# Three held chunks of the expert table turned by VectorE instead of TensorE

## The chip, the cores and the metric

The kernel runs on one core of a Trainium2 chip. The core has five engines, each with its own instruction queue worked strictly in order: TensorE (PE in the profile; its weight loads are PEld), VectorE (DVE), ScalarE (ACT), GpSimd (POOL) and SyncE (SP, which here only issues transfers). Transfers (DMAs) run beside them on 16 DMA engines; those that SP and ACT issue use hardware queues (q1 and q10), those of POOL a software queue (q0). The metric is the device time of one execution in microseconds, compared by medians of several executions on one chip.

## The reference

One decoder layer on 256 tokens of width 1024. The part before the experts (norm, one wide projection, retention, block attention, gates, output projection) is only touched by this change at its end. What matters is the expert step (PEER):

```python
def peer(h, w_q, sub_keys, u_tab, v_tab):
    q = (ht @ w_q).reshape(T, PEER_HEADS, 2, half)
    s = jnp.einsum('thcd,hcnd->thcn', q, sub_keys)
    s1, i1 = lax.top_k(s[:, :, 0], PEER_TOPK)
    s2, i2 = lax.top_k(s[:, :, 1], PEER_TOPK)
    ...                                   # 256 sums per token and head, top 16 of them
    gates = jax.nn.softmax(top_s, axis=-1)
    u = u_tab[ec]                         # 16384 experts, rows of 1024 numbers
    a = jax.nn.gelu(jnp.einsum('td,thkd->thk', hc, u), approximate=False)
    return jnp.einsum('thk,thkd->td', gc * a, v_tab[ec])
```

Each token needs 8 heads x 16 experts out of 16384. Everything is float32.

## The kernel before, in words

The program is written out in the order in which each engine is to work; nothing is reordered later. It has four stages.

**Mixer (to about 245 us).** The dense part of the layer, as a list of weight pieces of 512 KB. For piece i, SP loads it into a ring of six buffers (`raw_ring`), ACT and DVE cut it into a high and a low part (`cut`, L151 and L152), and PE multiplies (`products`). During this stage 28 of the 128 chunks of the expert table u (128 experts each, 512 KB) are already prepared: POOL loads a chunk as four quarters of its columns (`load_quarters`, L738, four DMAs of 128 KB each), DVE turns it with two block transposes (`turn`, L742), and ACT's queue stores it turned to memory (`turned`). These are the chunks in `EARLY`.

**Queries (about 245 to 300 us).** 16 more pieces, of `peer_w_q`, go through the same ring, cut three pieces ahead of their products. After every fourth piece the epilogue `queries(q)` runs: ACT copies the result (L612), PE multiplies it with the sub-keys (L625), ACT copies the scores (L629), and a top-k job for each half of the tokens is put on a list (`chain`), whose steps DVE works off in small portions between the cuts: `MAX8`, `FIND_INDEX8`, `MATCH_REPLACE8` (L905 to L914) and then the choice of the best 16 sums (L939 to L993). SP loads in this stage also the 14 chunks of `HELD` (`hold`, L1160) into the part of the large tile `W` that is still free, one for each piece, and the last three after the loop. In the epilogue of the fourth query block, between ACT's copies and the sub-key products, the program turns chunks 0 and 1 by `transpose_u` (`TAHEAD` = 2).

**Stage U (about 300 to 633 us).** For each chunk c of 128 experts, PE multiplies the turned chunk with the hidden states of 128 tokens (L1321, 16 matmul records a chunk) into `acc`. A chunk that is not in `EARLY` is first turned by PE (`transpose_u`, L728: eight 128x128 transposes into PSUM, copied out by ACT, L729), two chunks ahead. Because a block transpose by VectorE leaves the columns in another order, there are two copies of the hidden states: `hTf` for chunks that PE turns, `hTd` for those that VectorE turned; `early_chunk(c)` chooses. The other tokens are served in another way: POOL gathers single rows of u by index (L1050) and DVE multiplies them out (L1061). All the top-k steps that are left run on DVE in this stage too, between those products. When the second half of the tokens is done, ACT takes exponentials of their gates (L1007), DVE normalises them (L1012 to L1014), and PE turns the indices and gates (L1210), from where on DVE builds one-hot matrices for PE (L1188, L1191, L1246, L1247).

**Stage V (633 us to the end).** The weighted sum over the table v, chunk by chunk.

At the border between mixer and queries POOL issues, in this order: the result of the mixer to memory (L571), 64 rows of the normed states to `h2x` (L599), a shift of rows inside `h2` (L600), and four DMAs that spread `h2x` into `h2y` (L604), which ACT's queue loads at the begin of stage U (L1303).

Of the kernel before, what the change touches and what calls it, by code (L numbers as in the profile page):

```python
# [25 lines left out]
D = 1024  # L26
# [23 lines left out]
TOPK = 16  # L50
HELD = [0, 1, 2, 8, 14, 21] + list(range(26, 62, 6)) + [61, 66]
HELD0 = 2
FOLD = 104
TURNED = list(range(8, 36, 2)) + [37, 40, 42, 45, 47, 50, 52, 55, 57, 60, 62, 65, 67, 70]
NPRE = len(TURNED)
# [24 lines left out]
def layer_kernel(ctx, tc, x, mix_norm_g, w_in, ret_w_branch, moba_q_gain, moba_k_gain, moba_w_branch,  # L80
# [48 lines left out]
    def add(gen, front=False):  # L129
        tasks.insert(0, gen) if front else tasks.append(gen)  # L130
# [9 lines left out]
    def pump(n=3):  # L140
        for g in list(tasks)[:n]:
            if g in tasks:
                advance(g)
# [65 lines left out]
    def cut(i, engine=V):  # L209
        if i < len(pieces):  # L210
            hi, lo = hi_tile(), lo_tile()
            split_to(hi, lo, raws.pop(i), engine)
            splits[i] = (hi, lo)
# [333 lines left out]
    def residual(j):  # L547
        def epi(o):
# [50 lines left out]
            nc.gpsimd.dma_start(h2x, h2[P - NX:])  # L599
            nc.gpsimd.dma_start(h2[NG:], h2[:NG])  # L600
            yield
            for n in range(NXG):
                src = h2x[NXP * ((n - NXV) % NXG):][:NXP]
                nc.gpsimd.dma_start(h2y[n].rearrange("h i d -> i h d"), src[:, None, :].to_broadcast([NXP, H, D]))  # L604
                yield
        return epi

    def queries(q):
        def epi(o):
# [119 lines left out]
                A.activation(u_T[c][:, 512 * q:512 * (q + 1)], p, AF.Copy)  # L729

    def early_chunk(c):
        return c in EARLY

    def load_quarters(queue, dst, c, quarters=range(4)):

        src = peer_u[0, c * P:(c + 1) * P, :].rearrange("(b a) (g d) -> g a b d", a=32, g=4)
        for g in quarters:
            queue.dma_start(dst[32 * g:32 * g + 32].rearrange("a (b d) -> a b d", b=4), src[g])  # L738

    def turn(dst, src, k):  # L740

        V.transpose(dst.rearrange("p (k b a) -> p b k a", k=KC, b=4)[:, :, k],  # L742
                    src.rearrange("p (b k i) -> p b k i", b=4, k=KC)[:, :, k])
# [410 lines left out]
    V.tensor_copy(iota4, iota[:, :, None].to_broadcast([P, NK, 4]))  # L1154
    held = list(HELD)

    def hold():
        n0, c = 1024 * (len(HELD) - len(held)), held.pop(0)
        u_raw[c] = W[:, HELD0:SCRATCH, :].rearrange("p c t -> p (c t)")[:, n0:n0 + D]
        nc.sync.dma_start(u_raw[c], peer_u[0, c * P:(c + 1) * P, :])  # L1160

    for i in range(n_mixer + 3, len(pieces)):
        load_to(i + 1)
        if held and i > n_mixer + 4:
            hold()
        products(i)
        cut(i + 3)
        pump()
        chain_step(BUDGET_Q)

# [312 lines left out]
```

## Time and profile before

| | us |
|---|---|
| median of 3 runs | 932.54 (932.08 to 933.26) |
| time of the profiled execution | 930.49 |
| its span | 928.7 |
| PE busy | 919.9 (99%) |
| DVE busy | 801.3 (86%) |
| ACT busy | 510.5 (55%) |
| POOL busy | 450.3 (48%) |
| DMA | 333.03 MB, mean 359 GB/s |

The span runs from the first to the last instruction; the time of the same execution is 1.8 us longer. In rows of the profile an operation stands as `out<-in`, with buffer numbers where a row is of one buffer alone; idle time of an engine before an instruction stands in brackets with what ended it.

### The profile page before, as it was taken

The numbers are of one execution on the slowest core, as the hardware profiler recorded it, in microseconds if no ns is written. First come the engines' busy times: TensorE is split into PE (matmuls) and PEld (weight loads), VectorE is DVE, ScalarE is ACT, GpSimd is POOL, SyncE is SP. The second block draws the span as 40 slices with busy tenths as digits, with TensorE's granted clock in tenths as the row PEclk, the third lists the DMA queues.
The fourth block names the chain that finished last, engine by engine and source line by source line (L and its number), as shares of the span: only waits on it lengthen the run. The fifth ranks groups of instructions, "written<-read, shape, count | busy, mean of one in ns | idle before, by whom it ended". The sixth has DMA issues, their size and how long they took to land.

```text
span 928.7 us, 18726 instructions
## 1 busy us (share of the span) xinstructions
PE 919.9 (99%) x6952; PEld 873.5 (94%) x6952; DVE 801.3 (86%) x1539; ACT 510.5 (55%) x938; POOL 450.3 (48%) x420
## 2 busy tenths in 40 slices
PE   9999999999999999999999999999999999999998
PEld 6877888888999999999999999999999999999997
DVE  6578766888779999999999999975998989898896
ACT  5455654544654445344677777775454545454543
POOL 3627332321202447435576787873656554455540
PEclk9999999999999999999999999999999999999999
DMA  9999989999799999999999999999999999999991
GB/s 313 214 339 337 354 282 276 345 341 325 245 381 398 404 381 352 379 379 351 405 406 405 404 383 407 395 389 348 380 405 408 409 393 410 378 409 379 386 392 56
DMA packets 108265, 333.03 MB, mean 359 GB/s; under 512 B 12460, under 2 KB 16469, under 8 KB 108046
## 3 DMA queue, kind: packets, MB, share of 16 engines
q1 hardware_dynamic: 65532, 185.17, 54.6%
q0 software_dynamic: 37824, 129.57, 38.1%
q10 hardware_dynamic: 4818, 17.09, 4.8%
q8 instruction: 55, 0.90, 0.4%
q14 instruction: 36, 0.29, 0.1%
HBM read 313.88 MB, written 19.43 MB: 359 GB/s over the span
## 4 chain that ended last, share of the span: by engine, by line
PE 93%; DMA 5%; DVE 0%; issue 0%; ACT 0%; POOL 0%; SPq 0%; DVEq 0%; ACTq 0%
PE acc L1321 24%; PE side L728 10%; PE acc L1353 10%; PE side L1353 9%; PE acc L234 6%; PE acc L235 6%; PE acc L236 6%; PE acc L1354 4%; PE side L1354 4%; DMA raw_ring<-in_w_in_dram 3%; PE acc L244 2%; PE acc L243 2%; PE acc L245 2%; PE side L1351 2%; PE acc L1351 2%; PE acc L1246 1%
## 5 line engine op out<-in xcount | busy, mean ns | idle before, releaser
L1050 POOL DMA_INDIRECT rows<-in_peer_u_dram,eg x86 | 107.9, 1255 | 72.3 <-DVE rows L1061 26.4
L1050 POOL DMA_INDIRECT rows<-in_peer_v_dram,eg x54 | 97.8, 1812 | 77.2 <-DVE vacc L1149 58.8
L728 PE MATMUL side<-ident,raw_ring 128*128 128x128 f32 x688 | 92.3, 277 | 1.1 <-DMA raw_ring<-in_peer_u_dram 1.1
L728 PEld LDWEIGHTS side<-ident,raw_ring 128*128 128x128 f32 x688 | 83.3, 192 | 1.3 <-issue 1.3
L1293 ACT ACTIVATE cw<-W 128x352 fp32r<-128x352 f32 x58 | 28.9, 498 | 74.7 <-PE acc L1354 69.2
L1195 ACT ACTIVATE oh_buf<-oh_more,tS 128x128 bf16<-128x128 f16 x176 | 58.5, 417 | 0.0
L1061 DVE SCALAR_TENSOR_TENSOR rows<-rows,h 128x1024 f32<-128x1024 f32 x44 | 55.8, 1277 | 2.6 <-DMA rows<-in_peer_u_dram,eg 1.5
L1321 PE MATMUL acc<-hTd,raw_ring 128*128 128x128 f32 x448 | 54.6, 275 | 0.0
L1149 DVE SCALAR_TENSOR_TENSOR vacc<-rows,av,vacc 128x1024 f32<-128x1024 f32 x42 | 53.7, 1278 | 0.1
L1321 PEld LDWEIGHTS acc<-hTd,raw_ring 128*128 128x128 f32 x448 | 52.3, 192 | 0.0
L1294 DVE TENSOR_TENSOR cw<-W,cw 128x352 fp32r<-128x352 f32 x58 | 30.2, 521 | 21.3 <-ACT cw L1293 20.7
L1279 POOL TENSOR_TENSOR W<-W,gl 128x256 f32<-128x256 f32 (+21 forms) x32 | 28.1, 880 | 30.7 <-ACT gl L1278 26.7
L738 POOL DMA_DIRECT2D eraw<-in_peer_u_dram x40 | 21.9, 554 | 37.7 <-DVE eT L742 37.7
L738 POOL DMA_DIRECT2D h<-in_peer_u_dram x40 | 21.8, 552 | 37.7 <-DVE hTf L742 29.6
L1191 DVE TENSOR_TENSOR oh_buf<-oh_more,tM 128x1024 f16<-128x1024 f16 x44 | 33.2, 754 | 0.0
L1188 DVE TENSOR_TENSOR oh_more<-iota,tI 128x1024 f16<-128x1024 f16 x44 | 32.8, 746 | 0.0
L1262 ACT ACTIVATE W<-acc 128x512 f32<-128x512 f32 (+22 forms) x44 | 17.4, 394 | 13.6 <-PE acc L1247 9.6
L1246 PE MATMUL acc<-oh_buf 128*128 128x128 bf16 x176 | 24.4, 219 | 0.0
L1247 PE MATMUL acc<-oh_buf 128*128 128x128 bf16 x176 | 24.4, 219 | 0.0
L1281 ACT ACTIVATE W<-acc 128x256 f32<-128x256 f32 (+21 forms) x53 | 18.4, 348 | 5.5 <-issue 3.3
L1264 DVE TENSOR_TENSOR W<-acc,W 128x256 f32<-128x256 f32 (+21 forms) x32 | 16.1, 502 | 4.6 <-ACT W L1262 4.2
L1246 PEld LDWEIGHTS <-oh_buf 128*128 128x128 f16 x176 | 19.8, 114 | 0.0
(2599 smaller groups left out, 3391.9 us busy)
## 6 DMA issues: line engine op xcount, KB each, us to landing
raw_ring<-in_peer_v_dram SPq DMA_DIRECT2D x100, 512.0 KB
raw_ring<-in_peer_u_dram SPq DMA_DIRECT2D x86, 512.0 KB
raw_ring<-in_w_in_dram SPq DMA_DIRECT2D x52, 512.0 KB
raw_ring<-turned SPq DMA_DIRECT2D x28, 512.0 KB
W<-in_peer_v_dram SPq DMA_DIRECT2D x28, 512.0 KB
raw_ring<-in_peer_w_q_dram SPq DMA_DIRECT2D x16, 512.0 KB
W<-in_peer_u_dram SPq DMA_DIRECT2D x14, 512.0 KB
eraw<-in_peer_u_dram POOLq DMA_DIRECT2D x40, 128.0 KB
```

What stands on the lines that cost most here:

```text
L234: T.matmul(o[t], xh[:, s], wh, start=(k == 0), stop=False)
L235: T.matmul(o[t], xh[:, s], wl, start=False, stop=False)
L236: T.matmul(o[t], xl[:, s], wh, start=False, stop=(k == kc - 1))
L728: T.transpose(p[:, k * P:(k + 1) * P], r.rearrange("p (i k) -> p k i", k=KC)[:, 4 * q + k], ident)
L1050: G.indirect_dma_start(out=r, out_offset=None, in_=tab, in_offset=bass.IndirectOffsetOnAxis(ap=eg[:, j:j + 1], axis=0))
L1061: V.scalar_tensor_tensor(r, r, 1.0, h, op0=OP.mult, op1=OP.mult, accum_out=av[:, j:j + 1])
L1149: V.scalar_tensor_tensor(a, r, av[:, j:j + 1], a, op0=OP.mult, op1=OP.add)
L1195: A.activation(o1[:, j], hot[:, 0, :, j], AF.Copy, scale=tS[:, t, k + j:k + j + 1])
L1246: T.matmul(p[:, j * P:(j + 1) * P], hi, o1, start=True, stop=False)
L1321: T.matmul(pa[:, n:n + NA], uT[:, k * P:(k + 1) * P], hT[:, k], start=(c % 2 == 0 and k == 0), stop=(k == KC - 1), skip_group_check=True)
L1353: T.matmul(o[b][:, :2 * ND], vh[:, n], w, start=(c == 0), stop=False, skip_group_check=True)
L1354: T.matmul(o[b][:, :ND], vl[:, n], w[:, :ND], start=False, stop=(c == NK - 1), skip_group_check=True)
```

## The change

The first three chunks of `HELD` (0, 1 and 2) become `HTURN`. They are no longer loaded whole by SP and turned by PE. POOL loads each as four quarters of columns into a scratch region of `W` (two such regions, used in turn), DVE turns it with two block transposes into the place in `W` where the held chunk stood before, and PE uses it there with `hTd`. Quarters of chunks 0 and 1 are issued before the loop over the query pieces; those of chunk 2 inside the loop, after chunk 0 has been turned out of the region. The turns stand in the loop's first three steps, right behind the cut. The four DMAs into `h2y` move from the end of the mixer to the loop's tasks, and so behind the twelve quarters on POOL's queue. `hold` runs on SP for the other eleven chunks, from the same step of the loop on, and nothing of it is left after the loop.

```diff
--- before.py
+++ after.py
@@ -50,6 +50,7 @@
 TOPK = 16
 HELD = [0, 1, 2, 8, 14, 21] + list(range(26, 62, 6)) + [61, 66]
 HELD0 = 2
+HTURN = HELD[:3]
 FOLD = 104
 TURNED = list(range(8, 36, 2)) + [37, 40, 42, 45, 47, 50, 52, 55, 57, 60, 62, 65, 67, 70]
 NPRE = len(TURNED)
@@ -599,11 +600,13 @@
             nc.gpsimd.dma_start(h2x, h2[P - NX:])
             nc.gpsimd.dma_start(h2[NG:], h2[:NG])
             yield
-            for n in range(NXG):
-                src = h2x[NXP * ((n - NXV) % NXG):][:NXP]
-                nc.gpsimd.dma_start(h2y[n].rearrange("h i d -> i h d"), src[:, None, :].to_broadcast([NXP, H, D]))
-                yield
         return epi
+
+    def spread_rows():
+        for n in range(NXG):
+            src = h2x[NXP * ((n - NXV) % NXG):][:NXP]
+            nc.gpsimd.dma_start(h2y[n].rearrange("h i d -> i h d"), src[:, None, :].to_broadcast([NXP, H, D]))
+            yield
 
     def queries(q):
         def epi(o):
@@ -729,7 +732,7 @@
                 A.activation(u_T[c][:, 512 * q:512 * (q + 1)], p, AF.Copy)
 
     def early_chunk(c):
-        return c in EARLY
+        return c in EARLY or c in HTURN
 
     def load_quarters(queue, dst, c, quarters=range(4)):
 
@@ -1154,10 +1157,29 @@
     V.tensor_copy(iota4, iota[:, :, None].to_broadcast([P, NK, 4]))
     held = list(HELD)
 
-    def hold():
+    def held_tile():
         n0, c = 1024 * (len(HELD) - len(held)), held.pop(0)
         u_raw[c] = W[:, HELD0:SCRATCH, :].rearrange("p c t -> p (c t)")[:, n0:n0 + D]
+        return c
+
+    def hold():
+        c = held_tile()
         nc.sync.dma_start(u_raw[c], peer_u[0, c * P:(c + 1) * P, :])
+
+    def held_raw(j):
+        n0 = 2048 + 1024 * (j % 2)
+        return scratch[:, n0:n0 + D]
+
+    def hold_quarters(j):
+        load_quarters(nc.gpsimd, held_raw(j), held_tile())
+
+    def hold_turn(j):
+        for k in range(0, KC, 4):
+            turn(u_raw[HTURN[j]], held_raw(j), slice(k, k + 4))
+
+    for j in range(2):
+        hold_quarters(j)
+    add(spread_rows())
 
     for i in range(n_mixer + 3, len(pieces)):
         load_to(i + 1)
@@ -1165,6 +1187,11 @@
             hold()
         products(i)
         cut(i + 3)
+        j = i - n_mixer - 3
+        if j < len(HTURN):
+            hold_turn(j)
+            if j + 2 < len(HTURN):
+                hold_quarters(j + 2)
         pump()
         chain_step(BUDGET_Q)
 
```

POOL at the border between mixer and queries, before (`h` is the tile h2, `eg<-ei` the first list of experts for the gathers; in brackets what the instruction waits for, DMASW being POOL's own transfers):

```order
L600 DMA h_75<-h_75 64x1024 [waits DMASW3_49,DMASW7_49,DMASW2_49,DMASW0_49]
L604 DMA h2y<-h2x 16x8x1024 [waits DMASW1_49]
L604 DMA h2y<-h2x 16x8x1024 x3
L983 DMA eg<-ei 64x16 [waits DMAHW1_49,DVE_49,DMAHW3_49,PE_49,DMAHW6_49,Activation_49,Pool_49]
```

The same place after the change:

```order
L601 DMA h_75<-h_75 64x1024 [waits DMASW3_49,DMASW7_49,DMASW2_49,DMASW0_49]
L741 DMA W<-in_peer_u_dram 32x4x256 [waits DMAHW2_49,DMAHW3_49,DMAHW1_49,DMAHW4_49,DMAHW0_49,DMAHW5_49,DMASW1_49,DMAHW6_49,PE_49,DMAHW7_49,Activation_49,Pool_49]
L741 DMA W<-in_peer_u_dram 32x4x256 x4
L741 DMA W<-in_peer_u_dram 32x4x256 [waits DMASW6_49]
L741 DMA W<-in_peer_u_dram 32x4x256
L741 DMA W<-in_peer_u_dram 32x4x256 [waits DMASW0_49]
L741 DMA W<-in_peer_u_dram 32x4x256 [waits DMASW1_49,DVE_49]
L741 DMA W<-in_peer_u_dram 32x4x256 [waits DMASW2_49]
L741 DMA W<-in_peer_u_dram 32x4x256 [waits DMASW3_49]
L741 DMA W<-in_peer_u_dram 32x4x256 [waits DMASW4_49]
L608 DMA h2y<-h2x 16x8x1024 [waits DMASW5_49]
L986 DMA eg<-ei 64x16 [waits DMASW1_49,DVE_49]
```

Twelve DMAs now stand between the shift of rows and the spreading into `h2y`; the ninth, the first quarter of chunk 2, waits for DVE, that is for the turn of chunk 0.

DVE at the begin of the queries, before (the cuts of three query pieces, then the first top-k step):

```order
L1154 CAST iota_2373<-iota 128x512
L152 TENSOR_TENSOR rlo__2413<-raw_ring,rhi__2412 128x1024
L152 TENSOR_TENSOR rlo__2456<-raw_ring,rhi__2455 128x1024
L152 TENSOR_TENSOR rlo__2498<-raw_ring,rhi__2497 128x1024
L905 MAX W<-W 128x8 x2
L907 MAX_INDEX W<-W 128x8 x2
```

After the change:

```order
L1157 CAST iota_2369<-iota 128x512
L153 TENSOR_TENSOR rlo__2417<-raw_ring,rhi__2416 128x1024
L745 STREAM_TRANSPOSE W<-W 128x4x4x32 x2
L153 TENSOR_TENSOR rlo__2467<-raw_ring,rhi__2466 128x1024
L745 STREAM_TRANSPOSE W<-W 128x4x4x32 x2
L153 TENSOR_TENSOR rlo__2512<-raw_ring,rhi__2511 128x1024
L745 STREAM_TRANSPOSE W<-W 128x4x4x32 x2
L908 MAX W<-W 128x8 x2
L910 MAX_INDEX W<-W 128x8 x2
```

Six transposes are put between the three cuts and the first top-k step; each pair waits for the four quarters of its chunk.

PE at the end of the queries and the begin of stage U, before:

```order
L245 MATMUL acc<-hh,rlo__2809 128x256
L728 MATMUL side<-ident,W 128x128 x16
L625 MATMUL side<-skT,W 128x128 x8
L728 MATMUL side<-ident,W 128x128 x8
L1321 MATMUL acc<-hTf,rhi__2917 128x128 x8
```

After the change:

```order
L246 MATMUL acc<-hh,rlo__2827 128x256
L628 MATMUL side<-skT,W 128x128 x8
L1348 MATMUL acc<-hTd,W 128x128 x16
L731 MATMUL side<-ident,raw_ring 128x128 x8
```

The 24 transposes of chunks 0, 1 and 2 are gone, 16 of them from between the last query product and the sub-key products.

## The prediction

> **What bounds the kernel now.** I read the page first, its busy line and the shares of its chain of waits:
>
> ```profile
> PE 919.9 (99%) x6952; PEld 873.5 (94%) x6952; DVE 801.3 (86%) x1539; ACT 510.5 (55%) x938; POOL 450.3 (48%) x420
> PE 93%; DMA 5%; DVE 0%; issue 0%; ACT 0%; POOL 0%; SPq 0%; DVEq 0%; ACTq 0%
> ```
>
> TensorE sets the end, so 24 transposes less should show in full. An average can hide a second engine that is just as late in one stage. So I read busy times by stretch next (columns: length, then busy us and instructions of PE, PEld, DVE, ACT, POOL, then granted clock, DMA share, GB/s), and the waits of PE from 245 to 640 us and of VectorE from 262 to 449:
>
> ```profile
> 251.00:262.40 11.40, 11.40 (x100) 11.40 (x100) 3.92 (x5) 7.36 (x12) 2.65 (x5) 1.00 0.74 242
> 262.40:287.40 25.00, 24.93 (x204) 24.14 (x203) 21.86 (x81) 12.58 (x16) 0.55 (x1) 1.00 1.03 404
> 287.40:357.40 70.00, 70.00 (x625) 70.00 (x624) 67.85 (x292) 30.03 (x59) 33.03 (x33) 1.00 1.00 387
> 357.40:449.00 91.60, 91.60 (x824) 91.60 (x824) 90.74 (x333) 41.76 (x83) 44.08 (x42) 1.00 0.98 370
> 449.00:633.00 184.00, 182.88 (x1794) 182.71 (x1793) 164.18 (x280) 134.40 (x378) 132.55 (x110) 1.00 1.02 396
> ...
> PE side L728 <- DMA raw_ring<-in_peer_u_dram: 1.1, 1, 1.1
> ...
> DVE sm L1012 <- ACT gates L1007: 1.8, 1, 1.8
> DVE W L905 <- ACT W L629: 1.6, 1, 1.6
> DVE rlo__2592 L152 <- ACT rhi__2591 L151: 1.3, 1, 1.3
> DVE rlo__2758 L152 <- ACT rhi__2757 L151: 1.1, 1, 1.1
> DVE rlo__2809 L152 <- ACT rhi__2808 L151: 0.2, 1, 0.2
> DVE rlo__2550 L152 <- ACT rhi__2549 L151: 0.2, 1, 0.2
> ```
>
> In the two middle rows PE is busy 70.00 of 70.00 and 91.60 of 91.60 us, but VectorE too: 67.85 and 90.74. Between the end of the queries and 449 us it has one wait worth the name, 1.8 us. Where does PE next need VectorE? At the turn of the second half's gates:
>
> ```profile
> 357.50 0.29 DVE L1012 TENSOR_REDUCE sm<-gates 128x8 f32<-128x128 f32 x1 [1.76 <-ACT gates L1007]
> ...
> 448.50 0.29 DVE L1014 TENSOR_TENSOR gates<-gates,sm 128x128 f32<-128x128 f32 x1
> 449.23 0.14 PEld L1210 LDWEIGHTS side<-ident,gates 128*128 128x128 f32 x1
> ```
>
> VectorE ends the gates at 448.50 + 0.29 = 448.79 and PE loads them at 449.23: 0.44 us of slack after 200 us of work. So there are two chains to 449 us, PE's and VectorE's, equally long within half a microsecond. The change shortens the first and lengthens the second.
>
> **What PE saves.** Its transposes and the sub-key products around them, from the chain of waits:
>
> ```profile
> 282.17 0.71 PE side L625 x4
> 282.89 1.60 PE side L625 x12
> ...
> 296.00 1.81 PE side L728 x16
> 297.81 1.79 PE side L625 x16
> 299.59 0.88 PE side L728 x8
> ```
>
> Gone are 1.81 + 0.88 = 2.69 us. The 16 transposes also covered ACT's copy of the last query block: without them the 16 products should go as in the third block, 0.71 + 1.60 = 2.31 us instead of 1.79, which gives 0.52 back. PE's gain is 2.69 − 0.52 = 2.17 us, and 2.69 if nothing is given back. ACT's six copies behind those transposes go too, on an engine 55% busy: counted as nothing.
>
> **What VectorE gets.** The block transpose costs 0.70 us, and its pairs come where these rows stand:
>
> ```profile
> 70.14 0.70 DVE L742 STREAM_TRANSPOSE hTf<-h 128x512 f32<-128x512 f32 x1
> ...
> 259.54 1.23 DVE L152 TENSOR_TENSOR rlo__2498<-raw_ring,rhi__2497 128x1024 fp32r<-128x1024 f32 x1 [1.52 <-ACT rhi__2497 L151]
> 262.40 0.49 DVE L905 MAX8 W<-W 128x8 f32<-128x128 f32 x2 [1.63 <-ACT W L629]
> 265.06 1.23 DVE L152 TENSOR_TENSOR rlo__2550<-raw_ring,rhi__2549 128x1024 fp32r<-128x1024 f32 x1 [0.22 <-ACT rhi__2549 L151]
> 269.96 1.23 DVE L152 TENSOR_TENSOR rlo__2592<-raw_ring,rhi__2591 128x1024 fp32r<-128x1024 f32 x1 [1.33 <-ACT rhi__2591 L151]
> ```
>
> Six of them are 6 x 0.70 = 4.2 us, but before 262.40 VectorE is busy only 3.92 of 11.40 us, so the work itself would fit. The price is the wait: each pair stands until its chunk has landed, and everything behind it on this engine stands too: two cuts, the first top-k step at 262.40, and so the whole row up to 449 us.
>
> Call X the time at which the third pair ends. The top-k step starts at X instead of 262.40. Of that lateness VectorE's waits in the queries can absorb 0.22 + 1.33 + 1.12 + 0.23 = 2.90 us. The 1.76 at 357.50 is absorbed as well, since ACT's exponentials there follow PE's work. And 0.44 is slack at the gates. PE is therefore later at 449 us by X − 262.40 − 2.90 − 1.76 − 0.44 = X − 267.50, but never earlier than by 2.17. Behind 449 us PE is busy 182.88 of 184.00: a shift there reaches the end.
>
> **When the third pair ends.** POOL's queue, where the quarters go, with what follows a load of the same kind in the mixer:
>
> ```profile
> 249.18 0.61 POOL L599 DMA_DIRECT2D h2x<-h  x1 [2.81 <-DVE h L578]
> 252.68 0.52 POOL L600 DMA_DIRECT2D h<-h  x1 [2.88 <-DMA h2x<-h]
> 253.19 2.13 POOL L604 DMA_DIRECT2D h2y<-h2x  x4
> ...
> 28.57 2.26 POOL L738 DMA_DIRECT2D eraw<-in_peer_u_dram  x4
> ...
> 39.02 0.71 DVE L742 STREAM_TRANSPOSE eT<-eraw 128x512 f32<-128x512 f32 x1 [1.20 <-DMA eraw<-in_peer_u_dram]
> ...
> 73.31 2.19 POOL L738 DMA_DIRECT2D eraw<-in_peer_u_dram  x4
> ...
> 83.18 0.71 DVE L742 STREAM_TRANSPOSE eT<-eraw 128x512 f32<-128x512 f32 x1 [2.64 <-DMA eraw<-in_peer_u_dram]
> ```
>
> The first quarter takes the place of the first spreading DMA, 253.2. Let g be the time from a chunk's first quarter to its last one landed. Chunk 0 is turned g1 + 1.4 us later; only then is the scratch region free and the first quarter of chunk 2 issued (the ninth quarter waits for VectorE), and chunk 2 is turned g2 + 1.4 us after that. Chunk 1, issued beside chunk 0, ends between the two. X = 253.2 + g1 + 1.4 + g2 + 1.4 = 256.0 + g1 + g2: two loads in a row, the second one behind a turn.
>
> Bounds of g, with the page's row of GB/s in 40 slices of 23.2 us:
>
> ```profile
> GB/s 313 214 339 337 354 282 276 345 341 325 245 381 398 404 381 352 379 379 351 405 406 405 404 383 407 395 389 348 380 405 408 409 393 410 378 409 379 386 392 56
> ```
>
> From below: the transfer to h2x (256 KB) held POOL from 249.18 to 252.68, 3.5 us, with little beside it; if the fourth quarter, three issues of 0.55 later, needs as much, g = 1.65 + 3.5 = 5.15. From above: the two groups of the mixer for which VectorE stood waiting took 39.02 − 28.57 = 10.45 and 83.18 − 73.31 = 9.87. Chunk 0 is loaded while transfers run at 242 GB/s (share 0.74): I take a quarter of the way from 5.15 to 9.87, 6.3. Chunk 2 is loaded at 404 GB/s (share 1.03), more than any of the first ten slices of the span, which are the mixer, so it is nearer the upper rows: three quarters of the way, 8.7. X = 256.0 + 15.0 = 271.0, and the shift at the end is 271.0 − 267.5 = **+3.5 us**. Both at the lower bound give 266.3 − 267.5 = −1.2, both at 10.45 give 276.9 − 267.5 = +9.4.
>
> [...]
>
> PE also waits inside the queries, since the later cuts come late:
>
> ```profile
> 273.58 0.28 PE L245 MATMUL acc<-hh,rlo__2550 128*128 128x256 f32 x1
> 276.46 0.28 PE L245 MATMUL acc<-hh,rlo__2592 128*128 128x256 f32 x1
> ```
>
> The cut `rlo__2550` ended at 266.29, 3.67 us behind 262.40 once its 0.22 of waiting is gone: now at 271.0 + 3.67 = 274.7, 1.1 us after PE's 273.58. `rlo__2592` comes at X + 7.24 = 278.2, 0.7 later still. That is 1.8 us lost against 2.17 gained. It doesn't add to the 3.5: PE only arrives less early at the gates, where VectorE is last anyway.
>
> **What moves at no cost.** POOL issues 12 quarters, 12 x 0.55 = 6.6 us, and stands at the ninth for chunk 0's turn to about 260.9. Behind it are four quarters and the four spreading DMAs, issued by about 265. The latter are read by ACT's queue:
>
> ```profile
> 285.99 0.55 POOL L983 DMA_DIRECT2D eg<-ei  x1 [30.67 <-ACT W L629]
> 299.69 0.33 ACTq L1303 DMA_DIRECT2D rlo__2977<-h2y  x1
> ...
> 278.45 4.22 SPq L1160 DMA_DIRECT2D W<-in_peer_u_dram  x4
> ```
>
> POOL's next own work is at 285.99 and the read at 299.69, over 30 us after the issue. Were that cover gone, every microsecond would be one of ACT's. SP drops three loads, some 1.3 us apart in its last row, so the ring's first loads of u go out some 3.8 us earlier. PE's only wait for them is the 1.1 us, which may shrink or stay. The bytes are the same.
>
> **The sum.** −2.17 on PE, overtaken by VectorE's lateness: +3.5 at the end. The profiled execution takes 930.49 us (span 928.7), which becomes 934.0. It lies 2.05 below the median of the runs, 932.54, and I carry the difference: **936.0 us**.
>
> **Rivals.** A measurement of this kernel can tell about 0.2% from no change, 1.9 us.
>
> 1. *The quarters land like lone transfers and VectorE isn't late.* For the full gain X must stay under 265.3, g1 + g2 under 9.3, 4.7 each: a little under the lower bound of 5.15. For it: the light stretch at 242 GB/s. Against it: both measured groups. Time 932.54 − 2.17 = 930.4, faster; 0.16.
> 2. *Late, but just about evened out.* g1 + g2 between 9.6 and 13.4 puts the shift between −1.9 and +1.9. The lower bounds lie here (931.3). For it speaks that nothing but POOL's loads and SP's queue competes once the spreading has moved back; against it that the second load stands in a full stretch. Time about 932.5; 0.25.
> 3. *Both loads are as slow as in the mixer.* At 10.45 each X is 276.9; `rlo__2550` then comes at 280.6, PE loses 7.7 us in the queries, and VectorE is 9.4 late at the gates: 941.9; 0.12. For it: the rows of 10.45 and 9.87; against: the first load meets few others.
>
> **Chances.** The forecast, late by 1.9 to 7 us, has 0.47; its own range is 934.4 to 939.5. With rival 3 that is 0.59 for slower by more than 0.2%; rival 2 is 0.25 for within 0.2%, rival 1 is 0.16 for faster. The range that holds 8 in 10 reaches from 930.6, nearly the full gain, to 940.5, part of the way to rival 3.
>
> **What would show it.** VectorE standing before the second transpose of a later pair, ended by the quarters of `in_peer_u_dram`, and the first top-k `MAX8` near 271 instead of 262.4. PE waiting about 1 us for `rlo` near 274. VectorE's wait at the first `L1012` (357.50) gone. PE waiting for VectorE at the second half's gates by some 4 us (VectorE 3.9 later than before, PE 0.4 earlier, 0.44 of slack). 24 fewer records of the transposes. Wrong would be: `MAX8` before 266, with PE not waiting at the gates (then rival 1), or VectorE late and the gates on time, which would mean that its work up to 449 us isn't one unbroken row as I read it.

## The result

The change makes the kernel slower: 944.10 us median (941.81 to 945.08) against 932.31 for the kernel before on the same chip, a ratio of 1.0128 with a 95% interval of 1.0115 to 1.0141. That is +11.8 us, where +3.5 was forecast and 940.5 was the upper end of the range. The profiled execution took 943.64, its span is 941.9. Of all executions on record one was in the slow state (1113.73 us at a mean granted clock of 0.753, in the run `early_whole` below), and the ratios leave it out.

The busy line and the shares of the chain of waits of the changed kernel (line numbers are up to 27 higher than before):

```profile
PE 923.2 (98%) x6928; PEld 874.5 (93%) x6928; DVE 805.4 (86%) x1545; ACT 507.4 (54%) x932; POOL 452.8 (48%) x432
PE 71%; DVE 17%; DMA 9%; issue 1%; POOL 1%; ACT 1%; SPq 0%; DVEq 0%; ACTq 0%; POOLq 0%
```

There are 24 records less on PE and 6 more on DVE, as written. But PE's busy time has risen by 3.3 us, and of the chain that ended last 17% is now DVE and 9% DMA. The three turns and the first top-k step, in DVE's timeline, and the loads they wait for in POOL's:

```profile
255.67 1.23 DVE L153 TENSOR_TENSOR rlo__2417<-raw_ring,rhi__2416 128x1024 fp32r<-128x1024 f32 x1 [3.64 <-ACT rhi__2416 L152]
264.91 1.31 DVE L745 STREAM_TRANSPOSE W<-W 128x512 f32<-128x512 f32 x2 [8.01 <-DMA W<-in_peer_u_dram]
268.55 1.30 DVE L745 STREAM_TRANSPOSE W<-W 128x512 f32<-128x512 f32 x2 [1.23 <-DMA W<-in_peer_u_dram]
275.94 1.30 DVE L745 STREAM_TRANSPOSE W<-W 128x512 f32<-128x512 f32 x2 [4.99 <-DMA W<-in_peer_u_dram]
277.17 0.45 DVE L908 MAX8 W<-W 128x8 f32<-128x128 f32 x2
```

```profile
254.45 4.38 POOL L741 DMA_DIRECT2D W<-in_peer_u_dram  x8 [0.46 <-PE acc L246]
266.51 2.18 POOL L741 DMA_DIRECT2D W<-in_peer_u_dram  x4 [7.67 <-DVE W L745]
```

The first cut here stood at 254.88 in the profile of before:

```profile
254.88 1.23 DVE L152 TENSOR_TENSOR rlo__2413<-raw_ring,rhi__2412 128x1024 fp32r<-128x1024 f32 x1 [3.63 <-ACT rhi__2412 L151]
```

So 0.8 us of the 13.2 by which the two spans differ were there before the change could delay anything: POOL's transfer to `h2x`, ahead of the first quarter, is as late (249.97 against 249.18). VectorE stands for loads for 8.01 + 1.23 + 4.99 = 14.2 us, and the top-k step comes at 277.17 instead of 262.40. Then PE's waits from 245 to 640 us, and VectorE's from 262 to 465:

```profile
PE acc L246 <- DVE rlo__2567 L153: 5.0, 1, 5.0
PE side L731 <- ACT rhi__4678 L732: 3.3, 1, 3.3
PE acc L246 <- DVE rlo__2467 L153: 0.9, 1, 0.9
```

```profile
DVE W L745 <- DMA W<-in_peer_u_dram: 14.2, 3, 8.0
DVE rows L1064 <- DMA rows<-in_peer_u_dram,eg: 3.8, 2, 2.0
```

And where the lateness reaches PE for good, the gates of the second half. In this list `DVE gates L978` is a step of the choice of the best sums, and `L1015` and `L1017` are the steps that stood at `L1012` and `L1014` before:

```profile
367.12 0.28 DVE L1015 TENSOR_REDUCE sm<-gates 128x8 f32<-128x128 f32 x1
386.82 1.23 DVE L1064 SCALAR_TENSOR_TENSOR rows<-rows,h 128x1024 f32<-128x1024 f32 x1 [1.96 <-DMA rows<-in_peer_u_dram,eg]
455.52 0.31 ACT L1010 ACTIVATE gates<-gates 128x128 f32<-128x128 f32 x1 [7.26 <-DVE gates L978]
460.21 0.29 DVE L1017 TENSOR_TENSOR gates<-gates,sm 128x128 f32<-128x128 f32 x1
460.65 0.23 PEld L1237 LDWEIGHTS side<-ident,gates 128*128 128x128 f32 x1
```

PE loads the gates at 460.65 instead of 449.23, 11.4 us later; 10.6 without the mixer's 0.8. VectorE ends them 0.15 us before that. The wait of 3.3 us that PE shows is a little earlier: ACT stood 7.26 us for VectorE before its exponentials, and its copies of turned chunks stood behind them. Behind the gates another 1.8 us are added (span 941.9 − 460.65 = 481.2 against 928.7 − 449.23 = 479.5). So the lateness takes the way that was forecast. What has to be explained is its size.

### The profile page after: what moved, and what is told of

It is laid out like the page before. It is cut to its first block, busy times and chain, and to the rows that moved or that the text cites. A ratio compares the mean times of both kernels' runs of the same rounds, so it can differ in the third digit from the quotient of the medians.

```text
span 941.9 us, 18692 instructions
## 1 busy us (share of the span) xinstructions
PE 923.2 (98%) x6928; PEld 874.5 (93%) x6928; DVE 805.4 (86%) x1545; ACT 507.4 (54%) x932; POOL 452.8 (48%) x432
## 2 busy tenths in 40 slices
DMA packets 108409, 333.03 MB, mean 354 GB/s; under 512 B 12604, under 2 KB 16613, under 8 KB 108190
## 4 chain that ended last, share of the span: by engine, by line
PE 71%; DVE 17%; DMA 9%; issue 1%; POOL 1%; ACT 1%; SPq 0%; DVEq 0%; ACTq 0%; POOLq 0%
PE acc L1348 13%; PE side L1380 9%; PE acc L1380 9%; PE acc L235 6%; PE acc L236 6%; PE acc L237 6%; PE side L731 5%; PE acc L1381 4%; PE side L1381 4%; DVE rows L1064 4%; DMA rows<-in_peer_u_dram,eg 2%; DMA raw_ring<-in_w_in_dram 2%; DMA W<-in_peer_u_dram 2%; PE side L1378 2%; PE acc L1378 2%; DVE W L966 1%
## 5 line engine op out<-in xcount | busy, mean ns | idle before, releaser
L1053 POOL DMA_INDIRECT rows<-in_peer_u_dram,eg x86 | 105.7, 1229 | 74.3 <-DVE rows L1064 29.9
L1306 POOL TENSOR_TENSOR W<-W,gl 128x256 f32<-128x256 f32 (+21 forms) x32 | 25.5, 797 | 26.7 <-ACT gl L1305 24.6
L1215 DVE TENSOR_TENSOR oh_more<-iota,tI 128x1024 f16<-128x1024 f16 x44 | 36.0, 818 | 0.0
## 6 DMA issues: line engine op xcount, KB each, us to landing
W<-in_peer_v_dram SPq DMA_DIRECT2D x28, 512.0 KB, 10.6
```

The costliest lines, as they stand in the source:

```text
L1053: G.indirect_dma_start(out=r, out_offset=None, in_=tab, in_offset=bass.IndirectOffsetOnAxis(ap=eg[:, j:j + 1], axis=0))
```

## The experiments

Each time is a median. Each ratio is against the kernel before on the same chip; intervals are 95%. The kernel before was timed anew with each group of runs: 931.51 beside `turns_no_loads`, `row_groups`, `third_region` and `late`; 932.44 beside `early_whole`, `quarters_pe`, `late_fixed` and `late_holds`; 932.11 beside `rows32`, `cols128`, `two` and `before_again`; 932.47 beside the two with another order. Code cuts below are shortened; `...` or a text in angle brackets stands for what is left out.

| run | chunks come as | turned by | time | ratio |
|---|---|---|---|---|
| the kernel before | whole | PE | 932.31 | |
| `before_again` | whole | PE | 932.05 | 0.9997 (0.9982 to 1.0011) |
| `early_whole` | whole, ahead | PE | 932.78 | 0.9997 (0.9982 to 1.0012) |
| `cols128` | quarters of columns, 128 partitions | PE | 932.56 | 1.0005 (0.9996 to 1.0015) |
| `rows32` | quarters of rows, 32 partitions | PE | 936.18 | 1.0055 (1.0038 to 1.0071) |
| `quarters_pe` | the change's quarters | PE | 938.56 | 1.0062 (1.0040 to 1.0084) |
| `turns_no_loads` | not loaded | DVE | 931.64 | 0.9998 (0.9989 to 1.0008) |
| `two` | the change's quarters, two chunks | DVE | 935.42 | 1.0036 (1.0022 to 1.0050) |
| `late` | the change's quarters | DVE, later | 937.81 | 1.0069 (1.0053 to 1.0084) |
| `late_fixed` | the change's quarters | DVE, later | 940.39 | 1.0082 (1.0061 to 1.0103) |
| `late_holds` | the change's quarters | DVE, later | 939.00 | 1.0071 (1.0046 to 1.0096) |
| `late_0213` | quarters in another order | DVE, later | 938.63 | 1.0074 (1.0058 to 1.0091) |
| `third_region` | the change's quarters, all before any turn | DVE | 940.18 | 1.0081 (1.0065 to 1.0097) |
| the change | quarters of columns, 32 partitions | DVE | 944.10 | 1.0128 (1.0115 to 1.0141) |
| `order_0213` | quarters in another order | DVE | 944.71 | 1.0129 (1.0104 to 1.0154) |
| `row_groups` | groups of rows over 128 partitions | DVE | 955.01 | 1.0252 (1.0237 to 1.0267) |

### Are the transposes the cost, or the waiting?

```diff
 def hold_quarters(j):
-    load_quarters(nc.gpsimd, held_raw(j), held_tile())
+    held_tile()
+    if j < 2:
+        G.memset(held_raw(j), 0.0)
```

> The changed kernel without the twelve quarter loads: zeros are put into the two scratch regions, and the six transposes on VectorE stay where they are, with nothing to wait for (the three chunks are left out of the result). If the lateness is VectorE standing for the loads, the transposes fall into its idle time before the first top-k step: that step starts near 263, PE keeps its 2.2 us, the time is about 930 us (2 under the kernel before, 14 under the changed one). If the transposes themselves, or their place in VectorE's row, are the cost, the first top-k step starts some 4 us later than before, 267, and the time is about 932 to 934. If the order or the new copy of the hidden states costs something of its own, it stays near 944.

Measured: 931.64 us, no difference to the kernel before, and 12.5 us under the change. VectorE's timeline:

```profile
257.19 1.22 DVE L153 TENSOR_TENSOR rlo__2411<-raw_ring,rhi__2410 128x1024 fp32r<-128x1024 f32 x1 [3.63 <-ACT rhi__2410 L152]
258.33 1.30 DVE L745 STREAM_TRANSPOSE W<-W 128x512 f32<-128x512 f32 x2
260.66 1.29 DVE L745 STREAM_TRANSPOSE W<-W 128x512 f32<-128x512 f32 x2
263.00 1.30 DVE L745 STREAM_TRANSPOSE W<-W 128x512 f32<-128x512 f32 x2
264.71 0.49 DVE L908 MAX8 W<-W 128x8 f32<-128x128 f32 x2 [0.41 <-ACT W L632]
```

The top-k step comes 264.71 − 257.19 = 7.52 us after the first cut, as before (262.40 − 254.88 = 7.52), and it still waits 0.41 for ACT. The six transposes fit into idle time and cost nothing; the whole loss hangs on the loads. In this profile PE's gain is there, and of the size that was forecast. PE loads the gates at 449.41:

```profile
449.41 0.14 PEld L1239 LDWEIGHTS side<-ident,gates 128*128 128x128 f32 x1
```

That is 449.41 − 257.19 = 192.22 us behind the first cut, against 449.23 − 254.88 = 194.35 before: 2.13 us saved, where 2.17 were forecast. But at the end of the program 1.3 us are lost again: from SP's first output transfer to the last instruction it takes 7.7 us (922.06 to 929.8), before 6.5 (922.23 to 928.7). Over the whole program, counted from the first cut, 1.2 us are saved. The timed runs, with an interval of −1.0 to +0.7 us, can't tell that from nothing. Even with loads for nothing the change as it is written would have brought hardly more than 1 us.

### Is it the second load behind the first turn?

Chunk 2 gets a raw region of its own, the place of the last held chunk:

```diff
-for j in range(2):
+for j in range(3):
     hold_quarters(j)
 def held_raw(j):
+    if j == 2:
+        return <the place of the last held chunk>
...
-    if j + 2 < len(HTURN):
-        hold_quarters(j + 2)
```

> As the changed kernel, but chunk 2 has a raw region of its own (the place of the last held chunk, which is loaded later) and its four quarters are issued right behind those of chunk 1, before any turn. If the second load behind the first turn is what makes the third pair late, chunk 2 lands some 4 us behind chunk 1 (near 272), the third pair ends near 273 instead of 277.2, and the time is about 940. If the DMA engines are simply full, all twelve loads share them, chunks 0 and 1 land later for it, the third pair ends as before near 277 and the time stays near 944.

Measured: 940.18, the time that was expected for the serial load. All twelve quarters go out before any turn, nine at once and the last by 266.6, since the others wait on POOL for earlier ones to land. The top-k step comes 275.69 − 256.81 = 18.9 us after the first cut instead of 277.17 − 255.67 = 21.5:

```profile
256.81 1.22 DVE L153 TENSOR_TENSOR rlo__2421<-raw_ring,rhi__2420 128x1024 fp32r<-128x1024 f32 x1 [3.64 <-ACT rhi__2420 L152]
...
275.69 0.44 DVE L908 MAX8 W<-W 128x8 f32<-128x128 f32 x2
```

That is 2.6 us earlier, not the 4 that were expected: here the expectation's step was too large. Taking the serial load out saves 944.1 − 940.2 = 3.9 us (4.4 by the two ratios, since the chips differ). Some 8 are left.

> The changed kernel with two chunks instead of three: chunk 2 is held and turned as in the kernel before. The second pair ended at 269.8 in the changed kernel and the third cut takes 1.2, so the first top-k step starts near 271 instead of 277.2; eight quarters fill the DMA engines for less long. By VectorE's lateness alone the time is some 6 us under the changed kernel, 938; if the third load is only a third of the loss, 940; if the lateness were that of the first load alone, 943 or more.

Measured: 935.42, 2.6 us less than expected. Here the third chunk's load and turn are left to the old way (`HTURN = HELD[:2]`). So two chunks cost 935.42 − 932.11 = 3.3 us, and the third 8.5 of the 11.8. The first pair still waits 10.7 us for its load, with nothing of a third chunk in flight:

```profile
268.87 1.30 DVE L745 STREAM_TRANSPOSE W<-W 128x512 f32<-128x512 f32 x2 [10.72 <-DMA W<-in_peer_u_dram]
```

That is longer than the 8.0 of the change. Here the spreading DMAs into `h2y`, which the change has behind the third chunk's quarters, already go out from 261.1 on, beside these loads; whether they are the reason isn't separated. The profiled execution is also the slowest of the five (937.88).

### Is it enough to turn later?

Turns behind the fourth, sixth and eighth cut:

```diff
-if j < len(HTURN):
-    hold_turn(j)
-    if j + 2 < len(HTURN):
-        hold_quarters(j + 2)
+if j in (3, 5, 7):
+    hold_turn((3, 5, 7).index(j))
+    if j == 3:
+        hold_quarters(2)
```

> As the changed kernel with the same loads, but the turns stand further back in VectorE's row: behind the fourth, sixth and eighth cut of the queries instead of the first three, so that each load has landed when VectorE comes to it and the first top-k step isn't held up. If VectorE's standing is the whole loss, it has only the 4.2 us of transposes to take in, against 2.9 + 1.8 us of idle time and 0.4 of slack: the first top-k step starts near 263, PE isn't kept waiting at the gates, and the time is 931 to 932, at or a little under the kernel before. If the slow loads cost by themselves (other loads late, PE waiting for cut pieces), the time stays above 935.

> The run with late turns again, with chunk 2's place taken before the loop (there the third load had got another chunk's place, and the result was of wrong data, with the same number of transfers). Turns behind the fourth, sixth and eighth cut. By that run: about 937, with PE waiting some 3 us in the queries for pieces of w_q that land late behind the quarters, and 2 to 3 us at the gates.

Measured: 937.81 and, with the right place for chunk 2, 940.39. In the first, the third load went to another chunk's place. My expectation for it, 931 to 932, was wrong, and the second is 3 us above the 937 that I expected by then. In `late_fixed` no turn waits for a load any more, and still 8 of the 11.8 us are there. The waits of VectorE from 255 to 300 us in `late_fixed`, and PE's from 245 to 640:

```profile
DVE rlo__2662 L154 <- ACT rhi__2661 L153: 5.0, 1, 5.0
```

```profile
PE side L629 <- ACT W L616: 3.8, 1, 3.8
PE side L1240 <- DVE gates L1018: 1.0, 1, 1.0
```

VectorE now waits 5.0 us for ACT's cut of a query piece, and PE 3.8 for ACT. ACT itself waits for that piece (its waits from 250 to 305 us):

```profile
ACT rhi__2661 L153 <- DMA raw_ring<-in_peer_w_q_dram: 5.1, 1, 5.1
```

So the pieces of `w_q` that SP loads beside the quarters are late, and the form or the place of the loads costs something by itself, whoever turns.

```diff
-    if held and i > n_mixer + 4:
+    if held and i > n_mixer + 9:
```

> Late turns, and SP's held chunks begin five steps later, so that the pieces of w_q have nothing but the quarters beside them. If late pieces of w_q are what remains of the loss with late turns, they land in time now, VectorE waits for none of them, PE isn't kept waiting in the queries, VectorE comes to the gates about in time, and the time is 930.5 to 932. If the held chunks or the ring's first loads of u then come too late, PE waits for those at the begin of the expert step, and it stays at 935 or more.

Measured: 939.00, not the 930.5 to 932 that late pieces of `w_q` alone would have given, though its executions lie far apart (934.77 to 943.60, the fastest being the profiled one). In that profile VectorE's wait of 5.0 us is gone, PE waits only 1.0 for the gates, and 2.1 for the ring's loads of u, which come late now. Which wait makes the slower ones slow can't be read from one profile; as a whole the run says that moving other loads away doesn't pay.

### Place or form?

In these two kernels all loads of the three chunks are issued before the loop and the turns on VectorE are dropped. The loads of `early_whole`:

```diff
-        load_quarters(nc.gpsimd, held_raw(j), held_tile())
+        c = held_tile()
+        nc.gpsimd.dma_start(u_raw[c], peer_u[0, c * P:(c + 1) * P, :])
```

> The place of the loads without their form: the three chunks are loaded by GpSimd at the same point and ahead of the spreading, but each as one whole transfer of 512 KB into its held place, and TensorE turns them as in the kernel before; VectorE has no turns. If it is the place (1.5 MB put ahead of the query pieces, which used to come last), the pieces of w_q land 4 us later and the time is 934 or more. If it is the form of the quarters (DMA engines full at 220 to 270 GB/s instead of 400), whole loads run at 400 GB/s, PE isn't kept waiting in the queries, and the time is that of the kernel before, within 1 us.

> The form of the loads without VectorE's part: the twelve quarters are issued as in the changed kernel (all in one row, chunk 2's into its held place), TensorE then turns what lies there as in the kernel before, and no transposes are on VectorE (the three chunks stand in another order than they should, so their part of the result is wrong). If VectorE's standing is the whole loss, the time is that of the kernel before, about 932. If the slow quarters hold up the pieces of w_q behind them, the cut of the fifth or sixth query piece comes late, PE waits some 3 us in the queries, as in the run with late turns, and the time is 934 to 937; the difference to the run with whole loads is then the price of the form.

Measured: 932.78 for whole loads at the same place, no difference to before; 938.56 for the quarters, 1.6 above the range that was expected, though nobody turned them on VectorE. It is the form. The same 10 us of four kernels, by stretch (columns as in the prediction; last three: granted clock, DMA share, GB/s). Before:

```profile
258.50:268.50 10.00, 9.97 (x84) 9.77 (x84) 7.11 (x34) 4.16 (x7) 0.00 (x0) 1.00 1.03 396
```

The changed kernel:

```profile
258.50:268.50 10.00, 9.06 (x77) 8.86 (x76) 2.41 (x3) 4.12 (x6) 2.33 (x5) 1.00 1.04 267
```

Whole loads (`early_whole`), and the quarters without turns (`quarters_pe`):

```profile
258.50:268.50 10.00, 10.00 (x88) 10.00 (x87) 6.29 (x21) 4.88 (x7) 1.13 (x3) 1.00 1.01 386
```

```profile
258.50:268.50 10.00, 10.00 (x88) 10.00 (x86) 6.62 (x24) 4.55 (x7) 3.68 (x7) 1.00 1.05 240
```

The DMA engines are full in all of them, 1.01 to 1.05. But they move 240 to 267 GB/s where quarters are among the transfers and 386 to 396 where not. These stretches begin at the same time, though the first cut does not; 3.62 us behind each kernel's own first cut the 10 us carry 396, 277, 405 and 231 GB/s, with the same reading. Among quarters the engines are occupied longer for the same bytes, and those of others too: in these last stretches SP's transfers (q1) take 66.4% of the engines' time for 2.52 MB before and 51.6% for 1.19 MB in `quarters_pe`, 26% and 43% for each MB. PE waits 5.7 us for ACT in `quarters_pe`, and ACT for query pieces that come late (its longest wait for one):

```profile
PE side L628 <- ACT W L615: 5.7, 1, 5.7
ACT rhi__2703 L152 <- DMA raw_ring<-in_peer_w_q_dram: 5.8, 1, 5.8
```

With whole loads ACT waits for a query piece too, 3.5 us at most, but PE doesn't wait there.

### What in the form?

A quarter is both: pieces of 1 KB in memory, and a target of 32 partitions. Two kernels with TensorE's turns take one each; both give the right chunks in their usual place.

```diff
+    # rows32: 32 whole rows of 4 KB onto 32 partitions
+    nc.gpsimd.dma_start(u_raw[c][32*g:32*g+32], peer_u[0, c*P+32*g:c*P+32*g+32, :])
+    # cols128: 128 pieces of 1 KB onto 128 partitions
+    nc.gpsimd.dma_start(u_raw[c][:, 256*g:256*g+256], peer_u[0, c*P:(c+1)*P, 256*g:256*g+256])
```

> The run with whole loads, each of the three split into four transfers of 128 KB by rows: 32 whole rows of 4 KB onto 32 partitions, 12 transfers on GpSimd's queue, TensorE turns as in the kernel before. If the narrow target (32 partitions) makes the quarters slow, the 10 us from 258.5 carry some 240 to 270 GB/s with full engines, as with the quarters, and the time is 937 to 939. If it is pieces of 1 KB in memory, these run like whole loads, 386 GB/s, and the time is 932 to 933. If twelve issues on GpSimd's queue matter, it is in between.

> The counterpart: the same split by columns, 128 pieces of 1 KB onto all 128 partitions, 12 transfers of 128 KB, TensorE turns as before. If pieces of 1 KB are slow by themselves, 240 to 270 GB/s in the 10 us from 258.5 and a time of 937 to 939. If the narrow target alone is to blame, 386 GB/s and 932 to 933.

The same stretch of `rows32`, then of `cols128`:

```profile
258.50:268.50 10.00, 10.00 (x88) 10.00 (x87) 6.85 (x29) 4.36 (x6) 3.45 (x8) 1.00 1.05 260
```

```profile
258.50:268.50 10.00, 10.00 (x88) 10.00 (x87) 6.86 (x28) 4.35 (x6) 5.16 (x10) 1.00 1.03 366
```

Measured: 936.18, 0.8 under the range expected for a narrow target, and 932.56. Twelve issues of 128 KB on GpSimd's queue and pieces of 1 KB cost nothing that can be measured (932.56 against 932.11); with the target narrowed to 32 partitions the core moves 260 GB/s instead of 366, and the time rises by 4 us (5 by the ratio). By these two kernels the narrow target is the slow part of the form; why it is slow, no run shows. The 10 us with narrow transfers among others carry 240 to 267 GB/s, those without them 366 to 396. `quarters_pe`, which is both narrow and in pieces, is 2.4 us slower than `rows32` by the medians, on another chip; the intervals of their ratios overlap (1.0062 and 1.0055). Whether the pieces matter once the target is narrow, or chunk 2's other place, isn't separated.

```diff
+    load_quarters(nc.gpsimd, held_raw(j), held_tile(), (0, 2, 1, 3))
```

> The changed kernel with the four quarters of a chunk issued in the order 0, 2, 1, 3, so that neighbours on the queue go to partitions 0 to 31 and 64 to 95, then 32 to 63 and 96 to 127, instead of 0 to 31 and 32 to 63 first. If the slow form comes from two halves of the partitions that are reached by different ways, of which a row of quarters in order fills one at a time, two neighbouring transfers now run side by side, chunk 0 lands about 2 us sooner and the time falls to 937 to 941. If each transfer onto 32 partitions is slow whatever lies beside it, it stays at 943 to 945.

> The same order of quarters with the turns behind the fourth, sixth and eighth cut (940.4 with quarters in order). If the order lets two halves run side by side, pieces of w_q land sooner and the time falls to 934 to 938; otherwise 939 to 941.

Measured: 944.71 and 938.63. The order makes no difference in the changed kernel (ratios of 1.0129 and 1.0128), and with late turns, none that stands out of the intervals (1.0074 against 1.0082). Transfers to the two halves of the partitions, issued one behind the other, bring no time back in either.

```diff
-        load_quarters(nc.gpsimd, held_raw(j), held_tile())
+        dst = held_raw(j).rearrange("p (b d) -> p b d", b=4)
+        for b in range(4):
+            src = peer_u[0, c*P + 32*b:c*P + 32*b + 32, :].rearrange("a (g d) -> g a d", g=4)
+            nc.gpsimd.dma_start(dst[:, b], src)
```

> As the changed kernel, the same twelve loads of 128 KB, but each takes 32 whole rows of a chunk and spreads their four column quarters over all 128 partitions, instead of one column quarter onto 32 partitions. If the loads are slow because each is crowded onto 32 partitions (their packets of 4 KB took about 285 ns each, those of the queries' other loads 160), chunk 0 lands some 3 us sooner, 7 instead of 10.5 us after its first load, chunk 2 likewise, the first top-k step starts near 271 and the time is about 938. If it is the sharing of the DMA engines with SP's queue alone, nothing changes: step near 277, time about 944. If pieces of 1 KB are worse than the form of 4 KB, it is slower than 944.

Measured: 955.01, worse than the change, though each transfer reaches all partitions. I took that at first for a case against narrow targets; `rows32` and `cols128` settled it otherwise. The run isn't a clean one: the page's line of DMA packets of this kernel shows 1152 packets under 512 B more than the changed kernel's 12604, 96 for each of its 12 transfers, so that this form is carried out in another way. The two packet times in the expectation say less than they seem to: from 254 to 265 us the packets of q1, at some 160 ns, carry 2.5 KB on average (446 for 1.11 MB), so that for a byte they take nearly as long as the quarters' packets of 4 KB at 285.

```profile
DMA packets 109561, 333.05 MB, mean 351 GB/s; under 512 B 13756, under 2 KB 17765, under 8 KB 109342
```

### The second profile of before

> The kernel before once more, for a second profile: the mixer, which nothing of the change touches, ended 0.8 to 2.3 us later in the profiles of the changed kernels than in the one of the kernel before. If that is the scatter of executions, it ends anywhere in that span here too; if the change causes it, it ends near the first profile again.

Measured: 932.05; its first cut stood at 258.42, 3.5 us later than in the first profile of the same kernel. The mixer's end scatters by some 3.5 us from one execution to the next. The places of two profiles are to be compared from the first cut on. The end of the mixer is where they differ; from the first cut to PE's load of the gates both profiles of before take 194.35 us (449.23 − 254.88 and 452.77 − 258.42). By this measure the experiments part clearly, one profile each: 192.2 us in `turns_no_loads`, 194.4 in `early_whole`, 194.5 in `cols128`, 199.1 in `rows32`, 201.9 in `quarters_pe`, 205.0 in the changed kernel.

```profile
258.42 1.22 DVE L152 TENSOR_TENSOR rlo__2413<-raw_ring,rhi__2412 128x1024 fp32r<-128x1024 f32 x1 [3.64 <-ACT rhi__2412 L151]
```

No run beats the kernel before. The ones that come level don't use VectorE for the turn or don't load the chunks.

## Why the prediction was wrong

- **The direction, the way and the place: right.** VectorE stands for loads, the top-k row starts late, and the lateness reaches PE at the gates. `turns_no_loads` shows that the loads and not the 4.2 us of transposes are the cost, and that PE's gain was sized rightly (2.13 us for 2.17).
- **g1, the term that failed.** The step was: "Chunk 0 is loaded while transfers run at 242 GB/s (share 0.74): I take a quarter of the way from 5.15 to 9.87, 6.3." Measured: 264.91 − 254.45 = 10.46 us, the upper end. I read 242 GB/s as a light load beside which a quarter would be quick. But that row is an average from 251 to 262.4, and the load lasts from 254.5 to 264.9. In shorter stretches the kernel before shows where the light part lies:

```profile
251.00:254.40 3.40, 3.40 (x31) 3.40 (x31) 0.24 (x1) 2.27 (x5) 1.73 (x4) 1.00 0.34 76
254.40:258.00 3.60, 3.60 (x33) 3.60 (x33) 2.42 (x2) 2.89 (x6) 0.92 (x2) 1.00 0.78 246
258.00:261.00 3.00, 3.00 (x27) 3.00 (x27) 1.25 (x2) 1.51 (x3) 0.00 (x0) 1.00 1.00 363
261.00:264.90 3.90, 3.90 (x36) 3.90 (x35) 2.44 (x16) 2.31 (x3) 0.00 (x0) 1.00 1.03 393
```

  The light part (76 GB/s at a share of 0.34) is over before the first quarter goes out, and from 258 on the engines are full with SP's loads and the spreading. In the changed kernel the quarters come in the place of the spreading, and the engines are full again from 258 on (a share of 1.05 to 261). So the rows 10.45 and 9.87 of the mixer should have been the value and not the bound. Not all of this is the narrow target: in `cols128`, whose quarters reach all partitions, the twelfth quarter goes out at 264.15. It waits for the fourth to land, if the waits are as in the order listed for the changed kernel, where the ninth waits for DMASW1, eight transfers behind the first, and the twelfth for DMASW4. So the load of chunk 0 took 264.15 − 255.07 = 9.1 us there, and 2.8 of the 4.2 us by which g1 was too small are there too:

```profile
255.07 4.27 POOL L1177 DMA_DIRECT2D W<-in_peer_u_dram  x8 [0.44 <-PE acc L246]
264.15 0.54 POOL L1177 DMA_DIRECT2D W<-in_peer_u_dram  x1 [0.49 <-DMA W<-in_peer_u_dram]
```

  By the same reading it took 9.8 us in `rows32` and 12.2 in `quarters_pe`; how much of g1 is the form and how much the company therefore stays open.
- **g2: nearly right**, 275.94 − 266.51 = 9.43 against 8.7. The first quarter went out at 254.45, 0.5 later than by the sum (253.2 + 0.8 of mixer): it waits for PE's last use of the region.
- **X − 267.5: right as a rule, up to one new wait.** X without the mixer's 0.8 is 276.4, which gives +8.9 at the gates; measured are 10.6. VectorE's shift, with the 0.8, was 9.6 at `L1015` (367.12 − 357.50) and 11.7 at `L1017` (460.21 − 448.50). What came in between is a wait of 1.96 us for gathered rows (386.82) that the kernel before doesn't have. Without it the rule would have held within 0.3 us.
- **PE's waits in the queries**: forecast 1.1 and 0.7 for two later cuts. There was 5.0 for one of them, `rlo__2567`, which follows from X by the same sum (277.2 + 3.67 = 280.8, and PE went on at 280.74). A wait of 0.9 for `rlo__2467`, the cut behind the first pair, I hadn't seen. And PE's last wait, 3.3 us, stands at ACT's copies of a turned chunk, not at the gates themselves, where I had expected some 4.
- **The price of the form for others: missed.** I counted the twelve quarters as so many bytes and as issues on POOL at no cost. `quarters_pe` puts them at 6 us without VectorE having any part, by query pieces that land late. That in the changed kernel this lies under VectorE's longer standing, and that turning later, or freeing the second load, therefore gives back only about 4, is how I read it; no run separates the two there. What should have warned me was in the profile of before: in the stretch where the mixer's first quarters run (beside other small transfers) the engines are full, and move only 250 GB/s:

```profile
25.00:60.00 35.00, 34.18 (x169) 27.66 (x167) 20.28 (x25) 14.25 (x20) 17.47 (x22) 1.00 1.02 250
```

- **Rival 3**, both loads at 10.45, came nearest: 941.9, with a chance of 0.12. Rivals 1 and 2 fell with g1. Rival 1 needed 4.7 us for each load; beside other transfers the narrow ones of the changed kernel took 10.5 and 9.4, and the wide one of chunk 0 in `cols128` 9.1.
- **The end: a term that I had at nothing.** Of the lateness at the end 1.8 us come behind the gates, and all of it in the last microseconds: from the gates to SP's first output transfer it takes 472.8 us (460.65 to 933.47), before 473.0 (449.23 to 922.23), and from there to the last instruction 8.4 us instead of 6.5. In the ten profiles of kernels that turn on VectorE this last stretch takes 6.8 to 10.0 us, in the six others 6.4 to 7.1. In the last ten microseconds of each of the ten, and of none of the six, the view of the DMA queues shows a load of instructions on q8; in the changed kernel:

```profile
q8 instruction: 1, 0.02, 1.2%
```

  So it goes with the changed program. That this load is the cause would fit, but no run tests it.
- **In sum**: the forecast of 3.5, 4.2 for g1, 0.7 for g2 and 0.5 for the first quarter's later issue make the 8.9 at the gates. The new wait of 2.0, less 0.3 by which the rule was too high, makes 10.6, and the end's 1.8 makes 12.4. That is the 13.2 between the two spans without the mixer's 0.8.

## What to carry to other kernels

Before a load is given another form so that another engine can do the turning, look in the trace for loads of that form and take their pace as the price, also for whoever shares the engines: a DMA share near 1 says that the engines are busy, and GB/s beside it whether they are well used (here 1.05 at 260 GB/s in `rows32` and 1.03 at 366 in `cols128`). Take such a row for the time in which the load will run: an average that begins earlier hid full engines here (a share of 0.74 from 251 to 262.4, of 1.00 and 1.03 from 258 to 264.9). A wait put into an engine's row delays what stands behind it (here VectorE stood 14.2 us for loads and, without the mixer's 0.8, was still 8.8 us late at `L1015`, 90 us further on), so ask where that row next meets the bounding engine, and how many tenths of a microsecond lie there. And the gain of 2 us on the bounding engine needed both here: an engine beside it with room up to that meeting point, and transfers that are no slower than those they replace.

## What the runs showed of the hardware

- Transfers onto 32 partitions hold the DMA engines longer: 260 GB/s at a share of 1.05 with 32 whole rows of 4 KB, 366 at 1.03 with 128 pieces of 1 KB on all partitions (`rows32`, `cols128`).
- Behind both of its waits of 3 us and more between 245 and 640 us PE is slow for a while. The first products behind the wait of 5.0 us, and the granted clock in the stretches around PE's two long waits of the changed kernel:

```profile
280.74 0.58 PE L246 MATMUL acc<-hh,rlo__2567 128*128 128x256 f32 x1 [5.00 <-DVE rlo__2567 L153]
281.13 0.42 PE L244 MATMUL acc<-hh,rhi__2566 128*128 128x256 f32 x1
```

```profile
280.00:285.00 5.00, 4.26 (x24) 4.26 (x25) 5.00 (x29) 0.80 (x1) 0.00 (x0) 0.66 1.03 371
285.00:290.00 5.00, 5.00 (x44) 5.00 (x43) 4.93 (x23) 1.06 (x1) 0.00 (x0) 1.00 1.04 408
455.00:460.00 5.00, 3.63 (x22) 3.64 (x23) 4.86 (x15) 4.45 (x9) 2.91 (x3) 0.78 1.01 393
460.00:465.00 5.00, 5.00 (x42) 5.00 (x41) 3.09 (x7) 2.35 (x6) 4.01 (x4) 0.88 1.03 412
```

A product that took 0.28 us before takes 0.42, and the clock stands at 0.66 of full in 280 to 285, back at 1.00 from 285 on. In stretches of 1 us it is 0.50 from 281 to 283 and from 458 to 461, and by the stretches beside these each slow time lasts some 3.4 us. Behind PE's wait of 0.9 us (it goes on at 267.37) the clock stays at 1.00. Why it falls behind the long ones, and how long a wait has to be for it, isn't shown. The slow clock is part of why PE's busy time rose (919.9 to 923.2 us) while it did less. As an estimate from the stretches above, some (1 − 0.66) x 4.26 + (1 − 0.78) x 3.63 + (1 − 0.88) x 5 = 2.8 us of PE's time went into it. Most lies before the gates, where VectorE is last anyway. What lies behind them is some 0.3 us (460.65 to about 461.2), and it doesn't show any more at SP's first output transfer.
